# Retention in a hybrid trunk: values and gates of two heads in one product of 512 columns, and the first head's output transposes behind the next pair's query

## The chip, the core and the metric

The kernel runs on one core of a Trainium2 chip. A core has TensorE (PE, matmuls; its weight loads are shown apart as PEld), VectorE (DVE), ScalarE (ACT), GpSimd (POOL) and SyncE (SP, which here only issues transfers). The engines run side by side, each through its own instructions in order, and wait for each other by semaphores. SBUF is the working memory, PSUM the eight banks of 512 float32 a partition into which PE writes. The metric is the time of one execution on the device in microseconds (us).

## What is computed

The program is one inference step of a trunk of four layers (S5, retention, Hyena, S5) over 128 context tokens and 256 latent tokens, 1024 wide, in float32. The change lies in the retention layer alone, which has 8 heads of 128 query and key dimensions and 256 value dimensions:

```python
def retention_branch(h, s0, grid_pos, w_in, decay_logit, w_out):
    proj = h @ w_in                       # 1024 -> 1024 + 1024 + 2048 + 2048
    q, k, v, gate = jnp.split(proj, [RET_QK, 2 * RET_QK, 2 * RET_QK + RET_V], axis=-1)
    ...
    o_f, s_f = retention_chunkwise(q, k, v, lg[0], s0[:, 0], True)
    o_b, s_b = retention_chunkwise(q[:, ::-1], k[:, ::-1], v[:, ::-1], lg[1], s0[:, 1], False)
    o = o_f + o_b[:, ::-1]
    o = o * lax.rsqrt(jnp.mean(o * o, axis=-1, keepdims=True) + EPS)
    out = (o.reshape(bsz, L, RET_V) * jax.nn.silu(gate)) @ w_out
```

## The kernel before

All dense products are made in three parts: weights and activations are each split into a rounded value (h) and its remainder (l) of a reduced float32 type, and `mm` (L138 to L141) adds the products hh, hl and lh in PSUM. `unit` (L158 to L166) makes the two parts of 1024 weight elements a partition: ACT casts (L164), and the remainder is taken by POOL in one of three cases (through the helper at L136) and by DVE otherwise (L151). There are two buffers of each part. `weight` (L153 to L156) loads 1 MB on SP's queue into one of two buffers.

There are two ways to lay out a product. `featmajor` holds the weights in the array and moves 384 tokens through it: 24 matmuls a unit, one PSUM bank. `tokmajor` holds 128 tokens of the activation in the array and moves 256 weight columns through it, for three blocks of tokens at once: it takes all three banks of the pool `psd`, and a unit of 4 blocks of the contraction by 256 columns feeds 36 matmuls.

The retention layer goes through its heads in four pairs (`hp`). For a pair, queries and keys of both heads come first (four chunks by `featmajor`, `qk_chunk`), then values and gates by `tokmajor` (`vg_chunk`): value of the first head, gate of the first, value of the second, gate of the second, each with one 1 MB load and two units. A value is copied out of PSUM by ACT (L1086), a gate goes through a tanh on ACT (L533) and a product on DVE (L534) in `silu2`.

Between these chunks stand the steps of `head`: `scores` (products of q and k in two passes of float32, L1015 to L1023, masks by DVE into A, the key's transpose scaled into kk, L1020, and the loads of E, QD and the state s0 on SP's queue, L1006 to L1009); `values` (A times v and the scaled query times the state, L1031 to L1038, the norm's squares on ACT and its steps on DVE, L1043 to L1049, which write zt; and the new state from kk and v, L1053); and `turn` (six transposes of zt, L1061, copied by ACT into the blocks z that the output projection reads). kk, zt, s0 and QD have one buffer, the scores' A and E two. PSUM for these steps comes from the pool `psm` of four banks.

After each chunk stands a `tick`, which takes one task from a list of background work: one block of operators of the last S5 layer (`both`: expansions on DVE (L631, L632) and POOL (L636), small products L668 and transposes L674 into `psm`, and stores to scratch, among them that of CP, which has one buffer here), or nothing.

The second head's `values` and `turn` of a pair run behind the first two query chunks of the next pair (the list `late`), those of the last pair around the first steps of the output projection `OutProj`, which reads all blocks z.

The program's text isn't the order of execution: a planner goes through it with a model of times and takes for each engine the earliest instruction that is ready in the model, so that waiting chunks let later steps pass. On the chip each engine then keeps to the planned order.

Of the kernel before, what the change touches and what calls it, by code (L numbers as in the profile page):

```python
# [10 lines left out]
F32 = mybir.dt.float32  # L11
# [6 lines left out]
D = 1024  # L18
NB = D // 128
# [11 lines left out]
DV = 256  # L31
# [76 lines left out]
def hybrid_trunk(ctx: ExitStack, tc: tile.TileContext, I, O, dbg=None, layers=(0, 1, 2, 3)):  # L108
# [44 lines left out]
    def weight(src):  # L153
        raw = wraw.tile(list(src.shape), F32, tag="wr", name="wr")
        nc.sync.dma_start(raw, src)
        return raw  # L156
# [32 lines left out]

    def tokmajor(raw, act, epi):  # L190
        pss = [psd() for _ in range(3)]
        for k0 in range(0, NB, 4):
            w = unit(raw[:, k0:k0 + 4, :])
            for t in range(3):
                for kb in range(4):
                    mm(pss[t][:, :256], [p[:, k0 + kb, t * 128:(t + 1) * 128] for p in act],
                       [p[:, kb, :] for p in w], k0 + kb == 0, k0 + kb == NB - 1)
        for t in range(3):
            epi(t, pss[t][:, :256])

# [734 lines left out]
    def retention(i, zpool, hpool, nxt):  # L935
# [130 lines left out]
        for hp in range(4):  # L1066
# [15 lines left out]

            def vg_chunk(nm, m):
                o = vg[nm, m] = rot.tile([128, 3, DV], F32, tag=nm, name=nm)
                tokmajor(weight(W[(8 if nm == "v" else 16) + 2 * hp + m]), h,
                         lambda t, ps: S.copy(o[:, t, :], ps) if nm == "v" else silu2(o[:, t, :], ps))  # L1086

# [7 lines left out]
            if hp == 0:  # L1095
                z += [zblock(zpool, F32) for _ in range(16)]
            vg_chunk("v", 0)
            heads[0][0]()
            tick()
            vg_chunk("g", 0)  # L1100
            heads[1][0]()
            tick()
            vg_chunk("v", 1)
            heads[0][1]()
            tick()
            vg_chunk("g", 1)
            heads[0][2]()
            tick()
            late = [heads[1][1], heads[1][2]]
        drain()  # L1110
        op = OutProj(I["ret_w_out"], z, zpool, hpool)
        late[0]()
        op.split(0, 14)
        op.part(0, 0, 8)
        op.part(0, 8, 14)
        late[1]()
        op.part(1, 0, 8)
# [372 lines left out]
def _layout(a):  # L1490
    ca = np.ascontiguousarray
    o = {}
# [34 lines left out]
    qk = w[:, :2 * D].reshape(D, 16, 2, 2, 2, 16).transpose(0, 1, 2, 4, 3, 5).reshape(D, 2 * D)  # L1527
    o["ret_w_in"] = _slabs(np.concatenate([qk, w[:, 2 * D:]], 1), 256)
    o["ret_w_out"] = _slabs(a["ret_w_out"][0], 128)
# [48 lines left out]
```

## Time and profile before

| | us |
|---|---|
| median of three runs | 1631.56 |
| lowest and highest | 1630.19, 1633.9 |
| the profiled execution | 1632.28 |
| its span, first to last instruction | 1630.5 |
| PE, DVE, ACT, POOL busy | 1449.2, 1246.0, 692.2, 664.3 |

The busy time of PE counts a matmul from its start to its modelled end; matmuls overlap, so the distance from one start to the next is what a matmul costs in a stream. A wait in the views below is idle time of the waiting engine just before an instruction, named by what ended it; where a semaphore counts all instructions of an engine, the name may be that of a neighbour of the true cause. Retention's pairs run from about 456 to 757 us.

### The profile page before, as it was taken

The numbers are of one execution on the slowest core, as the hardware profiler recorded it, in microseconds if no ns is written. First come the engines' busy times: TensorE is split into PE (matmuls) and PEld (weight loads), VectorE is DVE, ScalarE is ACT, GpSimd is POOL, SyncE is SP. The second block draws the span as 40 slices with busy tenths as digits, with TensorE's granted clock in tenths as the row PEclk, the third lists the DMA queues.
The fourth block names the chain that finished last, engine by engine and source line by source line (L and its number), as shares of the span: only waits on it lengthen the run. The fifth ranks groups of instructions, "written<-read, shape, count | busy, mean of one in ns | idle before, by whom it ended". The sixth has DMA issues, their size and how long they took to land. (4 is left out here: it accounts for less than half of the span.)

```text
span 1630.5 us, 27608 instructions
## 1 busy us (share of the span) xinstructions
PE 1449.2 (89%) x10370; PEld 1280.7 (79%) x10370; DVE 1246.0 (76%) x2935; ACT 692.2 (42%) x1275; POOL 664.3 (41%) x484
## 2 busy tenths in 40 slices
PE   6778787798799899999979999999999999988996
PEld 3555585577588888889968988999998898767886
DVE  8966998699886767755968887888888874379565
ACT  2434522244333333334445544546445534542443
POOL 2111242325374857551225665655666332132221
PEclk9887899899799999999989999999999999999998
DMA  9487499843555555543333322322322345577531
GB/s 359 130 260 224 150 222 253 284 178 128 216 173 179 183 207 187 183 154 130 127 125 101 101 78 75 101 84 95 100 78 94 106 174 201 167 217 196 199 130 65
DMA packets 107805, 261.39 MB, mean 160 GB/s; under 512 B 28535, under 2 KB 68568, under 8 KB 88088
## 3 DMA queue, kind: packets, MB, share of 16 engines
q1 hardware_dynamic: 80768, 200.12, 37.2%
q0 software_dynamic: 11984, 34.87, 7.7%
q10 hardware_dynamic: 14920, 24.65, 4.3%
q8 instruction: 82, 1.34, 0.3%
q14 instruction: 51, 0.42, 0.1%
HBM read 220.37 MB, written 30.83 MB: 154 GB/s over the span
## 5 line engine op out<-in xcount | busy, mean ns | idle before, releaser
L136 POOL TENSOR_TENSOR wl<-wr,wh 128x1024 fp32r<-128x1024 f32 (+2 forms) x99 | 248.9, 2515 | 300.2 <-ACT wh L164 273.6
L164 ACT CAST wh<-wr 128x1024 fp32r<-128x1024 f32 (+4 forms) x211 | 215.7, 1028 | 315.0 <-PE psd L141 200.5
L141 PE MATMUL psd<-hh,wh 128*128 128x384 f32 x880 | 307.3, 350 | 13.5 <-DVE X L798 7.0
L141 PE MATMUL psd<-hl,wh 128*128 128x384 f32 x880 | 305.7, 347 | 6.4 <-DVE hl L472 6.2
L141 PE MATMUL psd<-hh,wl 128*128 128x384 f32 x880 | 305.3, 347 | 4.7 <-POOL wl L136 2.6
L151 DVE TENSOR_TENSOR wl<-wr,wh 128x1024 fp32r<-128x1024 f32 (+3 forms) x112 | 147.2, 1315 | 71.9 <-ACT wh L164 71.5
L141 PEld LDWEIGHTS psd<-hh,wh 128*128 128x128 f32 x880 | 169.7, 193 | 26.6 <-issue 14.5
L141 PEld LDWEIGHTS psd<-hl,wh 128*128 128x128 f32 x880 | 169.9, 193 | 15.9 <-DVE hl L472 8.9
L141 PEld LDWEIGHTS psd<-hh,wl 128*128 128x128 f32 x880 | 169.7, 193 | 12.2 <-issue 5.1
L141 PE MATMUL psd<-wl,hh 128*128 128x256 f32 x384 | 110.0, 288 | 4.0 <-POOL wl L136 2.0
L141 PE MATMUL psd<-wh,hh 128*128 128x256 f32 x384 | 110.0, 292 | 2.6 <-ACT k L1077 1.6
L141 PE MATMUL psd<-wh,hl 128*128 128x256 f32 x384 | 109.0, 286 | 0.0
L381 PE MATMUL psn<-wr,sgc 128*32 128x256 f32 x640 | 58.3, 460 | 35.0 <-DMA wr<-in_mod_w_dram 23.9
L141 PE MATMUL psd<-zb,wh 128*128 128x384 f32 x240 | 80.9, 338 | 0.0
L141 PEld LDWEIGHTS psd<-wl,hh 128*128 128x128 f32 x384 | 74.1, 193 | 6.3 <-POOL wl L136 3.2
L141 PEld LDWEIGHTS psd<-wh,hh 128*128 128x128 f32 x384 | 73.3, 193 | 4.5 <-ACT k L1077 2.0
L636 POOL TENSOR_TENSOR BP<-BP,xt 128x512 f32<-128x512 f32 x32 | 47.3, 1479 | 71.9 <-DVE xt L632 36.4
L141 PEld LDWEIGHTS psd<-wh,hl 128*128 128x128 f32 x384 | 74.1, 193 | 0.1
L631 DVE TENSOR_TENSOR CP<-B,xc 128x512 f32<-128x512 f32 x52 | 52.9, 1044 | 26.5 <-DMA scratch_cpd_dram<-CP 15.6
L632 DVE TENSOR_TENSOR xt<-BI,xc 128x512 f32<-128x512 f32 x52 | 47.2, 909 | 29.6 <-POOL CP L636 17.2
L381 PEld LDWEIGHTS psn<-wr,sgc 128*32 128x32 f32 x640 | 20.0, 124 | 56.9 <-DMA wr<-in_mod_w_dram 27.8
L797 DVE TENSOR_TENSOR X<-X,m 128x64 f32<-128x64 f32 x184 | 64.2, 349 | 0.0
(385 smaller groups left out, 3843.1 us busy)
## 6 DMA issues: line engine op xcount, KB each, us to landing
wr<-in_mod_w_dram SPq DMA_DIRECT2D x40, 1024.0 KB
wr<-in_hy_w_in_dram SPq DMA_DIRECT2D x32, 1024.0 KB
wr<-in_ret_w_in_dram SPq DMA_DIRECT2D x24, 1024.0 KB
wr<-in_s_w_in_dram SPq DMA_DIRECT2D x16, 1024.0 KB
wm<-in_mod_w_dram SPq DMA_DIRECT2D x8, 1024.0 KB
CP<-xt POOLq DMA_DIRECT2D x32, 256.0 KB, 7.2
Tt<-scratch_kd_dram SPq DMA_DIRECT2D x128, 64.0 KB
wr<-in_s_w_glu_dram SPq DMA_DIRECT2D x8, 1024.0 KB
```

The costliest lines, as they stand in the source:

```text
L136: G.tensor_tensor(out, a, b, op=op)
L141: TE.matmul(out, lhs[a], rhs[b], start=start and i == 0, stop=stop and i == len(combos) - 1)
L151: V.tensor_sub(out, a, b)
L164: S.copy(hi, ap)
L381: TE.matmul(ps[q * 32:(q + 1) * 32, :256], sg[:, kb, 6 - 2 * u:38 - 2 * u], raw[:, kb, :], start=u == 0 and k2 == 0, stop=u == 3 and k2 == 1)
L631: eng.tensor_tensor(out, c1, x[:, 0].unsqueeze(2).to_broadcast([128, 4, 8, 16]), op=OP.mult)
L632: eng.tensor_tensor(t, c2, x[:, 1].unsqueeze(2).to_broadcast([128, 4, 8, 16]), op=OP.mult)
L636: add.tensor_tensor(out, out, t, op=OP.add)
L797: V.tensor_add(dst, dst, m1[:, 0])
```

## The change

Values and gates are made for both heads of a pair at once. The weights' slabs hold 512 columns; a `tokmajor` chunk loads them in two halves of 1 MB, and a unit is 2 blocks of the contraction by 512 columns, which feeds 18 matmuls of 512 columns. There are two chunks a pair instead of four; v and g have one buffer of double width instead of two. The first head's scores stand ahead of the value chunk, the second head's behind it; the first head's values stand behind the gate chunk, and its `turn` moves to behind the first query chunk of the next pair. The four ticks stay four, one behind the value chunk, one behind the second head's scores, one behind the gate chunk, one behind the first head's values.

```diff
-    def tokmajor(raw, act, epi):
+    def tokmajor(src, act, epi):
         pss = [psd() for _ in range(3)]
-        for k0 in range(0, NB, 4):
-            w = unit(raw[:, k0:k0 + 4, :])
+        for k0 in range(0, NB, 2):
+            if k0 % 4 == 0:
+                raw = weight(src[:, k0:k0 + 4, :])
+            w = unit(raw[:, k0 % 4:k0 % 4 + 2, :])
             for t in range(3):
-                for kb in range(4):
-                    mm(pss[t][:, :256], [p[:, k0 + kb, t * 128:(t + 1) * 128] for p in act],
+                for kb in range(2):
+                    mm(pss[t], [p[:, k0 + kb, t * 128:(t + 1) * 128] for p in act],
                        [p[:, kb, :] for p in w], k0 + kb == 0, k0 + kb == NB - 1)
         for t in range(3):
-            epi(t, pss[t][:, :256])
+            epi(t, pss[t])
...
-            def vg_chunk(nm, m):
-                o = vg[nm, m] = rot.tile([128, 3, DV], F32, tag=nm, name=nm)
-                tokmajor(weight(W[(8 if nm == "v" else 16) + 2 * hp + m]), h,
-                         lambda t, ps: S.copy(o[:, t, :], ps) if nm == "v" else silu2(o[:, t, :], ps))
+            def vg_chunk(nm):
+                o = rot.tile([128, 3, 2 * DV], F32, tag=nm, name=nm, bufs=1)
+                for m in range(2):
+                    vg[nm, m] = o[:, :, m * DV:(m + 1) * DV]
+
+                def epi(t, ps):
+                    if nm == "v":
+                        S.copy(o[:, t, :], ps)
+                        return
+                    for m in range(2):
+                        silu2(vg[nm, m][:, t, :], ps[:, m * DV:(m + 1) * DV])
+                tokmajor(I["ret_w_vg"][hp + (0 if nm == "v" else 4)], h, epi)
...
-            vg_chunk("v", 0)
             heads[0][0]()
+            vg_chunk("v")
             tick()
-            vg_chunk("g", 0)
             heads[1][0]()
             tick()
-            vg_chunk("v", 1)
+            vg_chunk("g")
+            tick()
             heads[0][1]()
             tick()
-            vg_chunk("g", 1)
-            heads[0][2]()
-            tick()
-            late = [heads[1][1], heads[1][2]]
+            late = [heads[0][2], heads[1][1], heads[1][2]]
         drain()
         op = OutProj(I["ret_w_out"], z, zpool, hpool)
         late[0]()
+        late[1]()
         op.split(0, 14)
         op.part(0, 0, 8)
         op.part(0, 8, 14)
-        late[1]()
+        late[2]()
...
-    o["ret_w_in"] = _slabs(np.concatenate([qk, w[:, 2 * D:]], 1), 256)
+    o["ret_w_in"] = _slabs(qk, 256)
+    o["ret_w_vg"] = _slabs(w[:, 2 * D:], 512)
```

## Rows read from the trace of the kernel before

**Rows 1.** The page: engines' busy time, share of the span, instructions.
```profile
PE 1449.2 (89%) x10370; PEld 1280.7 (79%) x10370; DVE 1246.0 (76%) x2935; ACT 692.2 (42%) x1275; POOL 664.3 (41%) x484
```
**Rows 2.** Busy time by stretch: what follows the pairs, and all four pairs.
```profile
core 0: us, PE busy (x) PEld busy (x) DVE busy (x) ACT busy (x) POOL busy (x), PEclk, DMA share, GB/s
...
757.00:780.00 23.00, 23.00 (x132) 22.00 (x131) 15.17 (x31) 13.25 (x28) 6.49 (x7) 1.00 0.52 162
456.00:757.00 301.00, 279.29 (x2079) 258.49 (x2078) 206.25 (x375) 112.00 (x254) 173.97 (x129) 0.99 0.53 177
```
**Rows 3.** PE's groups, 456 to 757 us: count | busy us, mean ns | idle, releasers.
```profile
L141 PE MATMUL psd<-wl,hh 128*128 128x256 f32 x384 | 110.0, 288 | 4.0 <-POOL wl L136 2.0 <-DVE wl L151 1.9
L141 PE MATMUL psd<-wh,hh 128*128 128x256 f32 x384 | 110.0, 292 | 2.6 <-ACT k L1077 1.6 <-DVE g L534 1.1
...
L674 PE MATMUL psm<-ident,BP 128*128 128x128 f32 x112 | 16.7, 280 | 7.9 <-DVE A L1026 3.1 <-DVE kk L1020 2.2 <-DVE nr L284 1.1
```
**Rows 4.** PE's waits, 456 to 757 us: total us, times, longest.
```profile
PE psd L141 <- POOL wl L136: 4.6, 5, 1.5
PE psd L141 <- DVE g L534: 3.4, 4, 2.3
...
PE psd L141 <- DVE wl L151: 1.9, 2, 1.0
```
**Rows 5.** PE's timeline, 256 columns: start us, us, instruction.
```profile
573.13 0.28 PE L141 MATMUL psd<-wl,hh 128*128 128x256 f32 x1
...
574.57 0.28 PE L141 MATMUL psd<-wl,hh 128*128 128x256 f32 x1
```
**Rows 6.** PE's timeline, 384 columns.
```profile
599.63 0.33 PE L141 MATMUL psd<-hh,wh 128*128 128x384 f32 x1
...
601.19 0.33 PE L141 MATMUL psd<-hh,wh 128*128 128x384 f32 x1
```
**Rows 7.** PE's timeline, a head's values, each product two passes (x2).
```profile
577.97 0.59 PE L1038 MATMUL psm<-v,A 128*128 128x256 f32 x2
578.40 0.59 PE L1035 MATMUL psm<-s,qf 128*128 128x256 f32 x2
```
**Rows 8.** PE's timeline, its idle time in brackets with what ended it.
```profile
565.13 0.39 PE L141 MATMUL psd<-wh,hh 128*128 128x256 f32 x1 [0.30 <-DVE g L534]
...
595.69 0.44 PE L141 MATMUL psd<-hh,wh 128*128 128x384 f32 x1 [2.33 <-DVE g L534]
...
655.63 0.66 PE L674 MATMUL psm<-ident,BP 128*128 128x128 f32 x4 [2.24 <-DVE A L1026]
```
**Rows 9.** A gate's way out of PSUM, groups from 456 to 757 us.
```profile
L534 DVE SCALAR_TENSOR_TENSOR g<-silu,psd 128x256 f32<-128x256 f32 x24 | 9.5, 412 | 7.7 <-ACT silu L533 7.7
...
L533 ACT ACTIVATE silu<-psd 128x256 f32<-128x256 f32 x24 | 8.4, 379 | 9.7 <-PE psd L141 9.3 <-PE psm L1061 0.4
```
**Rows 10.** DVE's timeline, then PE's, at one late bank.
```profile
501.82 1.29 DVE L631 TENSOR_TENSOR CP<-B,xc 128x512 f32<-128x512 f32 x2 [4.20 <-DMA scratch_cpd_dram<-CP]
...
504.90 0.66 PE L674 MATMUL psm<-ident,BP 128*128 128x128 f32 x4 [1.86 <-DVE kk L1020]
```
**Rows 11.** PE's and DVE's timeline, from a head's values to its zt.
```profile
580.13 1.03 PE L1053 MATMUL psm<-v,kk 128*128 128x256 f32 x4
...
587.78 1.27 DVE L1049 SCALAR_TENSOR_TENSOR zt<-psm,rrs,g 128x256 f32<-128x256 f32 x3
```
**Rows 12.** The granted clock falls: one stretch, then PE's timeline.
```profile
620.00:622.00 2.00, 2.00 (x8) 2.00 (x8) 2.00 (x2) 0.13 (x1) 2.00 (x3) 0.50 0.90 360
...
618.33 0.44 PE L141 MATMUL psd<-hh,wl 128*128 128x384 f32 x1 [1.50 <-POOL wl L136]
...
620.35 0.52 PE L141 MATMUL psd<-hl,wh 128*128 128x384 f32 x1
620.67 0.52 PE L141 MATMUL psd<-hh,wl 128*128 128x384 f32 x1
```
**Rows 13.** SP's queue, 456 to 757 us: waits of the state's load.
```profile
SPq L1009 <- PE psm L1036: 19.1, 5, 9.5
```

## Prediction

> **What bounds the kernel now.** I read the page first: TensorE (PE) is busy 89% of the span, VectorE (DVE) 76%, the other two about 40% [rows 1]. An average over different stages says little about one stage, so the next view is the table by stretch. It is cut here at the four pairs of heads of the retention stage: from 456 to 757 us PE is busy 279.29 of 301.00 us, DVE 206.25, GpSimd (POOL) 173.97, ScalarE (ACT) 112.00, and from 757 on, when the output projection runs, PE is full [rows 2]. So in this stage PE sets the pace, and 21.7 us of it are idle. Third, PE's groups by shape: the 1152 matmuls with 256 moving columns are the largest item, 384 for each of three products of 110 us each; two of the three rows stand in [rows 3]. Those durations are no cost: a matmul lasts 288 ns in the trace, but the next starts long before it ends. What counts is the distance of starts, and for that one needs the timeline. Fourth, PE's waits in this stretch say where the idle 21.7 us lie [rows 4].
>
> **Part 1: 512 moving columns.** From 573.13 to 574.57 us twelve steps of 256 columns take 1.44 us, 120.0 ns a step [rows 5]. From 599.63 to 601.19 nine steps of 384 columns take 1.56 us, 173.3 ns [rows 6]. Both lie at full granted clock (2.4 GHz, 0.4167 ns a column): 256 columns are 106.7 ns and 384 are 160.0. The remainder is 13.3 ns in both, so it belongs to the instruction and not to the column. No matmul of 512 columns stands in the trace, so I extend the line: 213.3 + 13.3 = 226.7 ns, an estimate from those two rows. The change turns 1152 x 120.0 = 138.2 us into 576 x 226.7 = 130.6 us: **-7.7 us**. Bounds: a remainder of 2.9 ns, as of the retention's own two-pass products (0.433 us for two passes of 256 columns that move at two clocks a column, 216.3 ns each) [rows 7], gives 576 x (240.0 - 216.2) = -13.7 us; a remainder that doubles with the columns gives 0. I take the middle value, since its rows have the same line, operands and type.
>
> The Trainium skill says otherwise: "TensorE: Matmul & The Clock Gate", section "Back-to-back issue gap", gives N / 2.4 + 2.5 ns for a stream at full clock, and by an estimate from that the 256 columns would step in 109.2 ns, a pair of them would lose 2.5 ns by being joined, and the whole change would be worth 1.4 us. The trace disagrees at 256 and at 384 columns (120.0 and 173.3 ns), and the measurement decides for these; at 512 no run here shows which holds, so it returns as a rival.
>
> **Part 2: the weights' halves.** There are 32 units of 1024 elements as before, cast by ACT with the remainder by DVE or POOL as before, and 16 loads of 1 MB as before. A unit now feeds 18 matmuls, 4.08 us, instead of 36, 4.32 us. Where the unit's remainder comes late, that shorter stretch is no gain: PE just waits 0.24 us longer. Of the seven waits on remainders, 6.5 us in all [rows 4], 4.0 us stand ahead of 256-column products [rows 3], five of them at most; I give back 5 x 0.24 = **+1.2 us** (bounds 0 and 7.7, if every unit came late).
>
> **Part 3: fewer hand-overs of PSUM banks.** A chunk takes all three banks at once. PE waited 3.4 us in four times for a gate's evacuation [rows 4]. 1.1 us of that stand ahead of 256-column products [rows 3], that is at the border from the first head's gate to the second head's value; the row at 565.13 shows one of 0.30 [rows 8]. That border is gone: **-1.1 us**. The fourth, 2.33 us, stands between a gate chunk and the next pair's query [rows 8], and this border stays. There a bank now needs two tanh (379 ns) and two products (412 ns) instead of one each [rows 9], 0.8 us more; the first bank closes 12 x 0.2267 = 2.7 us ahead of the chunk's end, which hides that unless DVE is behind. The value's copies become half as many and twice as wide: nothing on the path, as ACT is busy 112 of 301 us [rows 2]. If each of the four gates ran into a wait of 2.33, this would be +7.0.
>
> **Part 4: scores ahead of the value chunk.** The first head's scores now come right behind the keys. They are some 1.2 us of PE (four passes of 256, two of 128 and a transpose), and they give ACT that much more to free the key's bank; PE waited 1.6 us there [rows 3]. I take half, **-0.8 us** (0 to -1.6). The scores' three loads (E, QD, s0) move on SyncE's queue, too: the first head's ahead of the value's weights, the second head's between value and gate. s0 has one buffer, so the second head's s0 waits for the first head's L1036, which now lies behind the whole gate chunk; queued behind it are the weights of the next pair's query. The queue waited so for 19.1 us in five times before, 9.5 at most [rows 13], and the view of PE's waits names no load [rows 4], as two weight buffers lie between: 0, and up to 9.5 a time if the query's weights were planned behind s0.
>
> **Part 5: what is bunched.** Four ticks of background work (a block of the last layer's operators each) still fall to the values and gates of a pair, but they come two by two with a head's step between, behind 16.3 us of matmuls, and no longer one by one behind 8.6 us. The transposes of that work (L674) need PSUM banks of the pool of four. PE waited 7.9 us there, for score products A 3.1, for kk 2.2, for a norm step 1.1 [rows 3]. Two things get tighter. kk has one buffer: the second head's kk must wait for the first head's state product (L1053), and until then its scores' bank is held. Between the two lay one chunk of 8.6 us, now one of 16.3. And DVE works in order: at 501.82 it had waited 4.20 us for the scratch store of CP before it could go on; kk stood behind that, and PE got its bank at 504.90, 1.86 us late [rows 10]. I take a quarter more of 7.9, **+2.0 us**, with bounds of -3 (the order comes out better) and +8 (all of it doubles).
>
> **Part 6: the transposes behind the next query.** For three pairs nobody reads z until the output projection: 0. They share zt with the second head, whose zt is written a chunk later. In the last pair the transposes stand at the end, behind the norm chain: state product from 580.13, zt until 589.05, about 8 us later [rows 11]. Beside it lie the second head's values (22 passes of 216 ns, 4.8 us), and the first 24 products of the output projection (24 x 0.1733 = 4.2 us), which read other blocks: 9.0 us. So 0, and 3.8 us if only one of the two covers it.
>
> **Sum.** -7.7 + 1.2 - 1.1 - 0.8 + 2.0 = -6.4 us. The profiled execution took 1632.28 us (span 1630.5), 0.7 above the median of 1631.56, so it is 1625.9 by that execution and **1625.2** by the median.
>
> **Rivals.**
> A. The remainder is not an instruction's. If only 2.9 ns, as of the two-pass products [rows 7], were the instruction's and the other 10.4 came again with every 256 columns, a product of 512 would take 213.3 + 2.9 + 20.8 = 237.0 ns, a gain of 3.0 x 576 = 1.7 us, and with the other terms (+1.3) the time would be about 1631.2. Against it: 256 and 384 columns have the same remainder. For it: nothing in the trace is wider than 386 columns, and at the lower clock level 384 columns step in 320 ns, 384 / 1.2 without any remainder [rows 12], so that it isn't an instruction's at all times. The rule of the Trainium skill's page named above would give nearly this time, too (1.4 us in place of 1.7).
> B. **The new bunches cost more than the matmuls give.** Place: DVE's queue behind each pair's value chunk, where CP of the second tick waits for the store of the first, and kk and the remainder stand behind. Price: the 4.20 us of [rows 10], not partly but wholly on PE, once a pair: 4 x 4.20 = 16.8, and 1625.2 + 16.8 = 1642. It decides from 6.4 / 4 = 1.6 us a pair, less than the 2.24 us that one such wait cost at 655.63 [rows 8]. For it: DVE is busy 69% of the stage and POOL 58% [rows 2]. Against it: the planner sees the same buffers and can put the two ticks apart.
> C. The remainder is smaller at 512 columns and less is bunched (+1.0 for part 5): -13.7 + 1.2 - 1.1 - 0.8 + 1.0 = -13.4, about 1618.
> D. A term of its own: soon after a wait of 1.50 us the granted clock stood at 0.50, its lower level of 1.2 GHz, from 620 to 622 us; 384 columns then step in 320 instead of 173.3 ns, so these 2 us hold 6.3 products instead of 11.5 and lose 0.9 us [rows 12]. Such a loss may vanish or come two or three times; it moves any case by that.
>
> **How the numbers follow.** Forecast 0.50 (1621 to 1629), A 0.13, B 0.20 (from little over 1632 to 1642), C 0.17. Of the forecast I count 0.43 beyond 0.2% (3.3 us, about what a measurement of this kernel can tell from no change) and 0.07 within; C is all beyond; A is within; of B 0.03 is within and 0.17 beyond. So faster 0.60, same 0.23, slower 0.17. The range goes from 1617 (C and a little) to 1637 (half of B's price); it leaves out some 0.07 below and 0.10 above.
>
> **What would show it.** Right: steps of 226 to 228 ns between 512-column products; 576 fewer matmuls; the stretch from the first value chunk to the output projection shorter by 5 to 8 us; PE's idle time in it about 22 us, with fewer waits on g. Wrong: steps of 216 (C) or 237 to 240 ns (A); waits of L674 on kk, A or a norm step of 15 us and more (B); PE idle at the start of the output projection, where it is full from 757 to 780 us now (part 6). If the sum fails, I expect it in part 5, whose size is the least known.

## The result, and the profile after

The changed kernel takes 1648.16 us (median of 4 runs, 1642.76 to 1654.99) beside 1632.39 for the kernel before (median of 4): a ratio of 1.0107, 95% interval 1.0082 to 1.0132. It is slower by 15.8 us where 6.4 less were forecast, and lies 11 us above the upper end of the range. Its profiled execution took 1654.99 us with a span of 1653.2; it is the slowest of the four, and 22.7 us longer than the profiled execution of the kernel before.

The page after: each engine's busy time, share of the span and instructions (beside [rows 1]):

```profile
PE 1457.7 (88%) x9794; PEld 1256.5 (76%) x9794; DVE 1251.1 (76%) x2935; ACT 692.9 (42%) x1263; POOL 670.9 (41%) x484
```

There are 576 matmuls fewer, as the change says (10370 to 9794), and yet PE is busy for longer. To see where, I cut the stage at landmarks that both kernels have. The *pairs* go from the first value product to the end of the last gate or value product; the *tail* from there to the start of the 110th `psd<-zb,wh` product of the output projection; the *rest* from there to the end. The table by stretch, first the kernel before, pairs and tail (start:end, length, then each engine's busy us and instructions, granted clock, DMA share, GB/s):

```profile
core 0: us, PE busy (x) PEld busy (x) DVE busy (x) ACT busy (x) POOL busy (x), PEclk, DMA share, GB/s
459.54:750.83 291.29, 269.58 (x2026) 249.25 (x2026) 197.00 (x360) 105.06 (x236) 170.68 (x126) 0.99 0.53 179
750.83:816.62 65.79, 65.50 (x366) 62.77 (x364) 54.05 (x97) 33.31 (x64) 14.30 (x14) 1.00 0.39 131
```

The same two stretches after:

```profile
461.44:756.00 294.56, 269.56 (x1447) 219.17 (x1446) 206.38 (x346) 102.69 (x216) 171.64 (x127) 0.97 0.53 177
756.00:834.93 78.93, 68.98 (x366) 65.23 (x367) 55.47 (x111) 35.14 (x72) 15.57 (x13) 0.91 0.32 109
```

Pairs and tail together are 373.49 us where they were 357.08: +16.4, about as much as the medians differ (15.8). (The two profiled executions differ by 6.3 us more, ahead of the stage and behind it.) Of the 16.4, +3.3 lie in the pairs and +13.1 in the tail, for the same 366 matmuls there. PE's idle time (length less busy) goes from 21.7 to 25.0 us in the pairs and from 0.3 to 10.0 in the tail: +12.9. The tail was the stretch where the prediction had PE full [rows 2].

The wide products themselves, groups of PE from 456 to 790 us (count, busy us, mean ns, idle time ahead of them; beside [rows 3]):

```profile
L141 PE MATMUL psd<-wl,hh 128*128 128x512 f32 x192 | 80.0, 417 | 6.8 <-DVE wl L151 4.6 <-POOL wl L136 2.1
L141 PE MATMUL psd<-wh,hh 128*128 128x512 f32 x192 | 73.3, 414 | 5.7 <-ACT wh L164 4.0 <-ACT k L1079 1.6
...
L676 PE MATMUL psm<-ident,BP 128*128 128x128 f32 x120 | 18.5, 283 | 0.3 <-DVE nr L287 0.3
```

and their distance, from PE's timeline, the first and the last of thirteen steps:

```profile
752.66 0.39 PE L141 MATMUL psd<-wh,hl 128*128 128x512 f32 x1
...
755.61 0.39 PE L141 MATMUL psd<-wh,hl 128*128 128x512 f32 x1
```

2.95 us for thirteen steps are 226.9 ns, as forecast. PE's waits, 456 to 790 us (total, times, longest; beside [rows 4]):

```profile
PE psm L1063 <- DVE zt L1051: 12.8, 2, 9.0
PE psd L141 <- DVE wl L151: 4.9, 6, 1.8
PE psd L141 <- DVE g L536: 4.1, 2, 2.7
PE psd L141 <- ACT wh L164: 4.0, 1, 4.0
PE psm L1033 <- DVE Kc L682: 2.3, 1, 2.3
PE psd L141 <- POOL wl L136: 2.1, 2, 1.4
```

The first line is new: L1063 are the transposes that the change moved. 9.0 us of the 12.8 are in the tail, the other 3.7 in the pairs:

```profile
720.37 0.48 PE L1063 MATMUL psm<-ident,zt 128*128 128x128 f32 x2 [3.73 <-DVE zt L1051]
```

PE's timeline in the tail (idle time in brackets, with what ended it):

```profile
751.57 1.02 PE L1055 MATMUL psm<-v,kk 128*128 128x256 f32 x4
...
756.37 0.45 PE L141 MATMUL psd<-zhh,wh 128*128 128x384 f32 x1 [0.38 <-ACT zhh L247]
765.85 0.69 PE L1063 MATMUL psm<-ident,zt 128*128 128x128 f32 x2 [9.03 <-DVE zt L1051]
766.33 1.06 PE L1033 MATMUL psm<-v,A 128*128 128x256 f32 x2
...
774.05 0.52 PE L141 MATMUL psd<-zb,wh 128*128 128x384 f32 x1
```

The transposes wait for zt at the head of PE's queue, and what should have covered that wait stands behind them: the second head's values (from 766.33) and the output projection (from 774.05, one product excepted). And zt is late because of ScalarE's queue in the same stretch:

```profile
755.81 2.16 ACT L247 CAST zhh<-zb 128x384 fp32r<-128x384 f32 x5 [0.51 <-PE psd L141]
757.88 0.64 ACT L535 ACTIVATE silu<-psd 128x256 f32<-128x256 f32 x2
758.42 1.33 ACT L247 CAST zhh<-zb 128x384 fp32r<-128x384 f32 x3
759.64 1.75 ACT L247 CAST zhl<-zb 128x384 fp32r<-128x384 f32 x4
761.29 0.83 ACT L164 CAST wh<-wr 128x768 fp32r<-128x768 f32 x1
762.03 0.38 ACT L535 ACTIVATE silu<-psd 128x256 f32<-128x256 f32 x1
762.30 0.38 ACT L1045 ACTIVATE junk<-psm 128x256 f32<-128x256 f32 x1
```

The squares (L1045), first link of the norm chain, run at 762.30, although the values that they read closed at about 751: six silu (the first three at 753.77 and 754.64), twelve casts for the output projection and a weight cast are planned ahead of them. VectorE ends the chain:

```profile
765.31 1.27 DVE L1051 SCALAR_TENSOR_TENSOR zt<-psm,rrs,g 128x256 f32<-128x256 f32 x3
```

**The clock** adds to that. The stretches of the stage with the lower of the two levels, 1.2 GHz, after:

```profile
495.25:498.75 3.50, 3.50 (x9) 2.75 (x10) 2.32 (x4) 2.02 (x3) 1.48 (x1) 0.52 0.90 251
625.00:632.00 7.00, 5.17 (x17) 3.69 (x20) 6.89 (x13) 1.32 (x2) 4.10 (x4) 0.51 0.25 96
679.75:683.00 3.25, 3.25 (x12) 3.25 (x12) 2.41 (x11) 1.51 (x8) 0.00 (x0) 0.50 0.39 103
720.75:724.00 3.25, 3.25 (x24) 2.08 (x24) 1.52 (x3) 1.31 (x4) 0.00 (x0) 0.50 0.31 48
758.25:771.75 13.50, 5.90 (x17) 4.91 (x18) 9.95 (x28) 7.40 (x23) 0.00 (x0) 0.50 0.07 21
```

and before (the first is that of [rows 12]):

```profile
619.25:622.75 3.50, 3.50 (x13) 3.50 (x12) 3.17 (x4) 0.28 (x1) 3.50 (x3) 0.52 0.91 300
656.75:660.25 3.50, 3.50 (x19) 3.50 (x18) 1.54 (x4) 1.21 (x2) 3.20 (x3) 0.51 0.71 253
```

If half of PE's busy time in these is lost, an estimate, that is 21.1 / 2 = 10.5 us after and 7.0 / 2 = 3.5 before. Together: idle +12.9, clock +7.0, and 16.4 - 12.9 - 7.0 = -3.5 is left for the work. So the wide products did give something, and two other things took more than five times as much.

### The profile page after: what moved, and what is told of

Read it like the earlier page. It is cut to its first block, busy times and chain, and to the rows that moved or that the text cites. A ratio compares the mean times of both kernels' runs of the same rounds, so it can differ in the third digit from the quotient of the medians.

```text
span 1653.2 us, 26440 instructions
## 1 busy us (share of the span) xinstructions
PE 1457.7 (88%) x9794; PEld 1256.5 (76%) x9794; DVE 1251.1 (76%) x2935; ACT 692.9 (42%) x1263; POOL 670.9 (41%) x484
## 5 line engine op out<-in xcount | busy, mean ns | idle before, releaser
L164 ACT CAST wh<-wr 128x1024 fp32r<-128x1024 f32 (+4 forms) x211 | 215.8, 1029 | 349.2 <-PE psd L141 218.8
L141 PE MATMUL psd<-wl,hh 128*128 128x512 f32 x192 | 80.0, 417 | 6.8 <-DVE wl L151 4.6
L141 PE MATMUL psd<-wh,hh 128*128 128x512 f32 x192 | 73.3, 414 | 5.7 <-ACT wh L164 4.0
L141 PE MATMUL psd<-wh,hl 128*128 128x512 f32 x192 | 77.0, 401 | 0.0
L638 POOL TENSOR_TENSOR BP<-BP,xt 128x512 f32<-128x512 f32 x32 | 50.8, 1587 | 60.2 <-DVE xt L634 39.1
L634 DVE TENSOR_TENSOR xt<-BI,xc 128x512 f32<-128x512 f32 x52 | 46.9, 904 | 26.8 <-POOL BP L638 12.8
L633 DVE TENSOR_TENSOR BP<-F,bc 128x512 f32<-128x512 f32 x64 | 55.0, 866 | 13.9 <-PE psm L676 11.7
L633 DVE TENSOR_TENSOR CP<-B,xc 128x512 f32<-128x512 f32 x52 | 48.6, 960 | 18.4 <-DMA xc<-in_s5bc_dram 11.4
L636 POOL DMA_DIRECT2D CP<-xt x32 | 27.9, 918 | 81.6 <-DVE xt L634 41.0
L634 DVE TENSOR_TENSOR xt<-FI,bc 128x512 f32<-128x512 f32 x64 | 50.7, 792 | 12.9 <-POOL BP L638 8.1
L638 POOL TENSOR_TENSOR CP<-CP,xt 128x512 f32<-128x512 f32 x32 | 46.2, 1445 | 34.8 <-DVE xt L634 22.5
```

Source lines behind the costliest of these rows:

```text
L141: TE.matmul(out, lhs[a], rhs[b], start=start and i == 0, stop=stop and i == len(combos) - 1)
L164: S.copy(hi, ap)
L633: eng.tensor_tensor(out, c1, x[:, 0].unsqueeze(2).to_broadcast([128, 4, 8, 16]), op=OP.mult)
L634: eng.tensor_tensor(t, c2, x[:, 1].unsqueeze(2).to_broadcast([128, 4, 8, 16]), op=OP.mult)
L636: nc.gpsimd.dma_start(out, t, accum_op=OP.add)
L638: add.tensor_tensor(out, out, t, op=OP.add)
```

## The experiments

Totals are a poor judge here: the stretch ahead of the stage, whose order of work is the same in all, took 452.9 to 466.8 us in 20 profiles. Pairs and tail repeat better (two profiles each of before, of the change and of e12 agree within 1.3, 1.8 and 3.0 us), so I read those first. All profiles, in us; "idle" is PE's in pairs and tail:

```
kernel             ratio to before, 95%      pairs   tail  idle   rest
before                                       291.3   65.8  22.0  813.9
b2_before_again    1.0004 (0.9977, 1.0030)   292.5   65.8  21.4  813.9
after              1.0107 (1.0082, 1.0132)   294.6   78.9  34.9  818.3
a1_changed_again   1.0137 (1.0102, 1.0171)   297.5   77.8  36.0  813.1
e1_move_only       1.0093 (1.0069, 1.0117)   298.0   67.7  25.5  815.0
e2_turn_back       1.0057 (1.0030, 1.0085)   283.9   77.5  27.8  816.9
e3_last_pair_old   1.0109 (1.0067, 1.0151)   295.9   67.7  26.7  816.7
e4_order_only      1.0088 (1.0053, 1.0123)   290.8   77.5  31.1  812.8
e6_later           1.0046 (1.0016, 1.0077)   294.7   72.3  29.1  813.6
e7_gf_later        1.0032 (0.9998, 1.0066)   285.9   75.9  27.2  815.6
e8_before_later    1.0056 (1.0029, 1.0084)   297.5   67.9  28.6  815.0
e9_ticks_spread    1.0087 (1.0055, 1.0118)   296.4   78.0  38.2  812.1
e10_all            1.0078 (1.0047, 1.0108)   286.0   75.8  28.1  812.3
e11_v_first        1.0096 (1.0064, 1.0128)   300.4   69.4  34.7  811.8
e12_both           1.0035 (1.0012, 1.0057)   284.9   67.6  21.1  820.9
e13_order_256      1.0022 (1.0001, 1.0043)   287.5   67.9  20.0  816.0
e14_tail_only      1.0032 (1.0010, 1.0055)   284.5   70.7  21.4  819.3
e15_gate_first3    1.0006 (0.9984, 1.0027)   287.3   67.8  21.5  814.6
e16_two_pairs      1.0057 (1.0032, 1.0083)   295.7   67.6  29.1  814.9
e17_both_again     1.0030 (1.0006, 1.0055)   287.6   67.9  21.5  817.6
```

The tails hold 360 to 375 products; those of e7 and e10 hold 389 (part of the first head's values falls behind the border), some 4 us of work that their pairs don't have.

### The two kernels again

a1 is the changed kernel unaltered, b2 the kernel before.

> The changed kernel once more, with a second profile, since its four times lie between 1642.8 and 1655.0 us and the trace read so far is that of the slowest. Theory T1 (the end of the stage): the wait of the first head's transposes in the last pair, 9.0 us in the first profile, stands in this one too, between 8 and 10 us, and the low clock behind it; what differs between the runs lies elsewhere. Theory T2 (bunched background work in the order of VectorE and ScalarE): the waits inside the pairs differ from run to run and sum up to more than the end. Time 1642 to 1655.

> The kernel before, unchanged: a second profile of it, to see how far the stage from the first value chunk to the output projection, its idle time and its low-clock time scatter from one execution to the next. The first profile had 357.6 us, 22.0 us and 6.8 us there. If these scatter by under 3 us, differences of 6 us between single profiles of variants carry weight; if by 6 or more, they don't. Time as before, ratio 1.000 within 0.003.

Measured: 1650.71 us and 1632.22 us. Pairs plus tail repeat within 1.8 and 1.3 us and idle time within 1.1 and 0.7, so a difference of 6 us between two profiles' stages counts.

### e1_move_only and e4_order_only: either half of the change with 256 columns

e1 is the kernel before with the transposes moved and nothing else:

```
-            heads[0][2]()
             tick()
-            late = [heads[1][1], heads[1][2]]
+            late = [heads[0][2], heads[1][1], heads[1][2]]
...
         late[0]()
+        late[1]()
...
-        late[1]()
+        late[2]()
```

e4 is the change with each joined chunk as two chunks of 256 columns, one behind the other (in short):

```
-                tokmajor(I["ret_w_vg"][hp + (0 if nm == "v" else 4)], h, epi)
+                for m in range(2): tokmajor(weight(W[(8 if nm == "v" else 16) + 2 * hp + m]), h, ...)
```

> The kernel before with 256 columns and four chunks, only the first head's transposes moved behind the next pair's first query chunk. In the last pair the second gate chunk (8.6 us) still stands between the first head's values and its transposes. T1: no wait at the end, 1632 (1630 to 1636, at most the 3.7 us that the moved transposes cost inside a pair). T2: 1632, as nothing is bunched. If the move itself were the loss: 1640 or more.

> The changed kernel's order (both values, then both gates, scores and ticks placed the same, transposes moved) with products of 256 columns, so 1152 matmuls at 120 ns. If the step per instruction is what the 512 columns save: the changed kernel + 7.7 us = 1656 (1650 to 1660). If the wide products themselves make the loss: 1632 to 1636. T1: a wait of some 9 us for the transposes at the end here too.

Measured: 1644.92 and 1642.60 us. e1 came out by its third case, that the move itself is a loss; e4 lies between its two. The table by stretch of e1 and its waits:

```profile
460.85:758.83 297.98, 274.54 (x2025) 255.44 (x2025) 211.69 (x360) 106.19 (x236) 174.51 (x126) 0.96 0.53 175
758.83:826.51 67.68, 65.61 (x366) 62.87 (x365) 54.03 (x97) 33.10 (x64) 15.03 (x14) 1.00 0.37 125
```
```profile
PE psm L1061 <- DVE zt L1049: 6.8, 2, 4.1
PE psm L674 <- DVE zt L1049: 4.5, 1, 4.5
...
PE psm L674 <- DVE nr L284: 3.1, 1, 3.1
```

The same two stretches of e4, and its transposes in the tail:

```profile
457.87:748.64 290.77, 268.36 (x2016) 247.18 (x2016) 210.30 (x347) 104.51 (x229) 168.34 (x128) 0.99 0.55 180
748.64:826.13 77.49, 68.85 (x375) 65.34 (x374) 57.18 (x111) 35.40 (x71) 15.41 (x14) 0.96 0.33 112
```
```profile
758.21 0.69 PE L1061 MATMUL psm<-ident,zt 128*128 128x128 f32 x2 [7.66 <-DVE zt L1049]
```

So the tail is lost without a single wide product (e4, 77.5), and it is nearly whole with the transposes moved but the chunks in their old order (e1, 67.7). With the moved transposes, what loses it is the order of the chunks: both heads' gates directly ahead of the first head's values, so that silu and casts stand ahead of the squares. And the move, which the prediction priced at nothing inside the pairs, costs 6.7 us there (298.0 against 291.3). Only 1.7 us of that is more idle time; 5.0 us is PE being busy for longer (274.54 against 269.58) at the lower clock, which covers 23.9 us of e1's pairs and 6.8 before.

### e3_last_pair_old and e2_turn_back: one part undone with 512 columns

e3 does the last pair in the order of the kernel before (256 columns), the other three as in the change (in short):

```
+            if hp < 3:
...
+            else:
+                vg_old("v", 0); heads[0][0](); tick(); vg_old("g", 0); heads[1][0](); tick()
+                vg_old("v", 1); heads[0][1](); tick(); vg_old("g", 1); heads[0][2](); tick()
```

e2 is the change with the transposes called at the pair's end again:

```
             heads[0][1]()
+            heads[0][2]()
             tick()
-            late = [heads[0][2], heads[1][1], heads[1][2]]
+            late = [heads[1][1], heads[1][2]]
...
```

> The changed kernel with the last of the four pairs done as before (four chunks of 256 columns, transposes at the pair's end). T1: the 9 us of waiting at the end and some 2.4 us of half clock behind it go, 1.9 us of matmul gain of that pair go too: 1648 - 11.4 + 1.9 = 1639 (1634 to 1643). T2: three of four pairs keep their bunches: 1648 - 16/4 = 1644 or more.

> The changed kernel with one part undone: the first head's transposes stand right behind its values again, at the end of the pair, in place of behind the next pair's first query products. In the last pair the order of TensorE's work comes out as in the changed kernel. Theory 1 (the transposes' wait for zt in TensorE's queue is the loss): the wait in the last pair of about 9 us stays, the one of 3.7 us inside the pairs goes or moves with the transposes; 1644 to 1650. Theory 2 (the bunched background work is the loss): nothing of it is changed, 1648 to 1650. So this run tells mainly whether the place of the transposes in the program text matters at 512 columns.

Measured: 1647.35 and 1643.49 us. e3's tail is 67.7 us, 11 less than the change's, as theory 1 said; its pairs stay at 295.9. (Its time does not show that: 1640.98 in the profiled run, 1647.35 in the median.) e2's tail stays at 77.5, and its pairs are shorter than in either kernel:

```profile
465.70:749.63 283.93, 266.14 (x1447) 216.74 (x1446) 208.74 (x346) 103.02 (x216) 170.65 (x127) 0.98 0.56 183
749.63:827.09 77.46, 67.50 (x367) 64.19 (x367) 55.38 (x111) 35.16 (x72) 15.58 (x13) 0.93 0.32 111
```

7.4 us less than before and 10.6 less than the change. That the transposes' place doesn't matter is out for the pairs. For the tail e2 says nothing about it: the planner brings the last pair's transposes to the same place there, PE's order through the tail is that of the change, and the wait is again 9.03 us. e14 below moves them in the tail.

### e6_later, e8_before_later, e7_gf_later: the transposes later still

If waiting for zt were the loss, more distance would repair it. All three write zt in place of the gates, so that each head has its own, and call the transposes later; e6 is so made from the change, e8 from the kernel before, e7 from the change with gate and value chunk exchanged:

```
-            late = [heads[0][2], heads[1][1], heads[1][2]]
+            late = [heads[1][1], heads[0][2], heads[1][2]]
...
+        op.split(0, 12)
+        op.part(0, 0, 8)
+        op.part(1, 0, 8)
         late[1]()
...
```

> The changed kernel with the first head's transposes later still: behind the next pair's second query products (zt is written in place of the gates, so that both heads have one of their own), and in the last pair behind the first 48 products of the output projection, whose blocks 0 to 11 are split first. The 512 columns and the bunched background work stay. Theory 1 (transposes wait for zt in TensorE's in-order queue, with matmuls behind them, and the low clock follows): waits on zt fall from 12.8 to under 2 us, and with some 4 us of low clock the time falls to 1630 to 1636. Theory 2 (bunched background work): waits on weights, gates and casts stay near 15 us and low clock too; 1643 to 1650.

> The kernel before (256 columns, its order of chunks) with the same later place of the first head's transposes. The move alone, to directly behind the first query products, gave 1644.9. Theory 1 (distance between the values and the transposes decides): 1629 to 1634, waits on zt under 2 us where the move alone had 11. Theory 2 (any new order of this stage lands some 10 us worse, whatever the transposes wait for): 1640 to 1646.

> As the run before it (transposes later), and the gate chunk ahead of the value chunk, so that the norm chain of the first head's values does not stand behind the six silu pairs on ScalarE and VectorE. Theory 1: waits on zt under 1 us, 1627 to 1634. Theory 2: background ticks fall at the same places, 1643 to 1650. If it comes out below the kernel before, the 512 columns' 3 to 8 us are seen.

Measured: 1639.43, 1642.15 and 1639.71 us. e8's time is theory 2's; those of e6 and e7 lie between the two. Theory 1 falls for the pairs. e8 shows no wait of the transposes at all and its pairs are 297.5 us, as long as e1's; e6's waits on zt are down to 3.8 us and its pairs are as long as the change's (294.7). e7's 285.9, with the gates first, is some 4 us too short by the border (see above): it comes to about 290. The idle time has moved to other waits: in e8 12.8 us on weights' remainders where [rows 4] has 6.5. So with the moved step the pairs are 3 to 6 us longer than before even where it waits little or not at all itself. That it changes what stands ahead of what on VectorE, ScalarE and POOL is my reading; no run isolates it (zt moved into the gates, too).

### e9_ticks_spread, e10_all, e11_v_first: part 5 of the prediction

e9 is the change with one tick in the middle of each joined chunk (`half` in its loop) and one behind each:

```
+            if half and k0 == 2:
+                half()
```

e10 is e7 with that, e11 is e6 with that.

> The changed kernel, only its ticks of background work put back to one per eight microseconds: one in the middle and one behind each joined chunk, in place of two by two behind each. The transposes stay where the change put them. Theory 1 (transposes waiting for zt): the waits on zt of 9 to 13 us stay and the time is 1646 to 1650. Theory 2 (bunched background work, part 5 of the prediction): waits on weights' remainders, gates and casts fall from 15 to 8 us, time 1636 to 1640.

> 512 columns with all suspects treated at once: ticks spread as in the run before, gate chunk ahead of the value chunk, transposes behind the second query products, and in the last pair behind the first 48 products of the output projection. If transposes' waits, bunched ticks and the silu ahead of the squares are the whole loss, the wide columns' own gain is left, some 4 us: 1626 to 1630. If merging the chunks costs in another way (weights' remainders, granted clock), it stays at 1636 to 1641, as with late transposes and gate first but bunched ticks (ratio 1.003).

> As the run before it, with the value chunk ahead of the gate chunk, as in the change. If the order of the two chunks matters by itself (six silu pairs between values and norm chain), 4 us slower than that run and waits on g of 3 us or more; if not, within 3 us of it.

Measured: 1644.56, 1642.82 and 1643.93 us. e9 keeps the waits on zt (9.7 us), as theory 1 has it; its waits on remainders, gates and casts fall from 15.1 to 11.8 us, but those on k rise from 1.6 to 6.9. e10 lies above both of its cases. Spreading the ticks gives the change nothing (374.4 us of pairs and tail against 373.5 and 375.3), nor e7 (361.7 against 361.8). e11's time is within 1.1 us of e10's, but its stage is 8 us longer; the order of the two chunks matters there.

### e12_both, e13_order_256, e14_tail_only: both losses undone

e12 is e2 in three pairs and e3 in the last. e13 is e12 with 256 columns, edited as e4, and so prices the columns. e14 is e2 in three pairs and e6 in the last, 512 columns throughout:

```
             heads[0][1]()
+            if hp < 3:
+                heads[0][2]()
             tick()
+            late = [heads[1][1]] + [heads[0][2]] * (hp == 3) + [heads[1][2]]
```

> 512 columns in the first three pairs, with the first head's transposes back at the pair's end, and the last pair wholly in the order of the kernel before (256 columns, single chunks). If the loss is the two places where transposes wait (inside the pairs and at the last pair), what is left is three quarters of the columns' gain: the pairs end some 6 us earlier than before, the end of the stage is as before; 1625 to 1628 by a median of 1631 for before. Rival (merging chunks costs in another way, seen in every variant so far at ratios of 1.003 to 1.01): 1635 to 1640.

> The run before it with 256 columns: two chunks of 256 one behind the other in place of each joined one, all else the same. If 227 against 2 x 120 ns a step is the whole of the columns' worth, 432 x 13.3 ns = 5.7 us longer than that run in the stage, so 1631 to 1634. If the joined chunks cost as much in waits as they give in steps, no difference.

> 512 columns in all four pairs, transposes back at the pair's end in three of them; in the last pair they stand behind the first 48 products of the output projection (zt is written in place of the gates). If the place of the transposes is the whole loss of the last pair, 1625 to 1629; if the silu work ahead of the squares and the values of both heads at the end cost by themselves (6 us more matmul and evacuation work is then behind the last chunk), 1632 to 1638.

Measured: 1634.74, 1634.94 and 1635.27 us: near the rival's case for e12, no difference for e13, the second case for e14. In e12 the stage is 4.6 us shorter than before, near what was expected, and the time is not. Pairs, tail and rest of e12, and the pairs of e17, which is e12 once more:

```profile
462.93:747.78 284.85, 265.78 (x1593) 223.66 (x1593) 212.91 (x360) 105.45 (x227) 169.30 (x126) 0.99 0.55 183
747.78:815.43 67.65, 65.62 (x368) 62.88 (x366) 53.80 (x97) 33.09 (x64) 15.02 (x14) 1.00 0.36 125
815.43:1636.30 820.87, 761.73 (x5173) 696.33 (x5172) 612.67 (x1312) 388.49 (x650) 346.82 (x220) 0.97 0.37 123
```
```profile
458.12:745.70 287.58, 268.36 (x1593) 226.72 (x1593) 212.46 (x360) 105.78 (x227) 168.90 (x126) 0.98 0.55 181
```

The pairs of e13, and the tail of e14:

```profile
462.94:750.40 287.46, 269.77 (x2025) 250.17 (x2025) 216.92 (x360) 106.16 (x236) 167.42 (x126) 0.99 0.54 182
```
```profile
740.58:811.30 70.72, 67.57 (x368) 64.16 (x366) 54.45 (x111) 34.77 (x72) 15.21 (x14) 0.98 0.34 119
```

At the same granted clock PE is busy 4.0 us less in e12's pairs: 432 wide steps in place of 864, 9.2 ns each, close to what the steps give. The pairs are only 2.6 us shorter than e13's, and those of e17, with more of the lower clock, not at all (287.58); e13's are 3.8 us shorter than before without any wide product. So most of what e12 gains in the pairs is the new order's, and what the columns give in length is not clear of the scatter.

e14 settles the tail. Its chunks stand as in e2, but zt is written into the gates, and in the last pair 48 products of the output projection are queued ahead of the transposes: no wait on zt is left in the tail, PE idles 3.2 us there in place of 10.0, and the tail is 70.7 us in place of 77.5. So the chunks' order makes zt late, and the transposes' place in PE's queue makes PE wait for it; the loss needs both.

Behind the stage e12 loses 7.0 us, at places that no edit touched. There PE's order is another one from the 99th instruction behind the tail on: the next layer's filter products stand earlier, and wait. PE's waits of e12 from 815 to 870 us:

```profile
PE psm L461 <- DVE dg L460: 5.2, 1, 5.2
PE psm L1267 <- ACT ab L1259: 2.3, 1, 2.3
```

Before has the first of these, too, but not the second.

### e15_gate_first3, e16_two_pairs, e17_both_again: was it the order behind the stage?

e15 is e12 with gate and value chunk exchanged in the first three pairs, e16 is e12 with only the first and the third pair joined; in both, PE's order behind the stage is that of the kernel before for over 4000 instructions. e17 is e12 once more. The edits of e15 and of e16 against e12:

```
-                vg_chunk("v")
+                vg_chunk("g")
...
-                vg_chunk("g")
+                vg_chunk("v")
```
```
-            if hp < 3:
+            if hp in (0, 2):
```

> 512 columns in three pairs with the gate chunk ahead of the value chunk in these, the transposes at the pair's end, the last pair as in the kernel before. TensorE's order behind the stage is that of the kernel before. If the new order behind the stage was what cost 7 us in the run with both repairs, then here the stage is 353 to 356 us, the remainder behind it 812 to 815, and the time 1626 to 1630. If the remainder is longer whatever its order, 1633 to 1636.

> The run with both repairs, with 512 columns in the first and the third pair alone. Order behind the stage as in the kernel before. 288 steps of 512 columns at 2 x 119.7 - 229.2 = 10.2 ns less give 2.9 us: stage 354 to 356, remainder 812 to 815, time 1628 to 1630; 1633 to 1636 if the order behind the stage is not the cause.

> The run with both repairs again, unchanged. If its stage and its remainder belong to the kernel and not to the one execution, 351 to 355 us and 817 to 821 us; time 1632 to 1637.

Measured: 1632.35, 1640.57 and 1636.27 us. The rest is 814.6 and 814.9 us with the old order, 820.9 and 817.6 with the new one. The other profiles, sorted by that order, agree: the nine with the order of before for over 4000 instructions (before, b2, e6, e8, e9, e11, e13, e15, e16) have 811.8 to 816.0 us behind the tail, the four with e12's (e3, e12, e14, e17) 816.7 to 820.9, and the seven with others (the change's among them, which part from before at about the 133rd instruction) 812.3 to 818.3. That makes e12's order worth some 4 to 5 us by the medians, where one and the same kernel scatters by up to 5.2 (the change). Of the mechanism the new wait is shown, 2.3 to 2.7 us in all four, and the clock (0.84 from 815 to 870 us in e12, where before has 0.91 in its 55 us there); the remainder I can't name. e15's stage and rest came out as expected for the old order, though its time lies between its two cases; e17 came out within 0.5 us of what was expected. e16 missed for another reason: its pairs take 295.7 us with 27.0 of idle time, though e12 has both kinds of pair, too. e15 is the best version found: 2.0 us shorter than before in pairs and tail, and in time the same as the kernel before (1.0006, 0.9984 to 1.0027). No version beat it.

## Why the prediction was wrong

**Part 1 was right in the step and some 2 us too large in its worth.** The step is 227 ns (median of the undisturbed ones), close to the forecast 226.7, and rival A with its 237.0 is out. The rule cited beside rival A, of the Trainium skill's "TensorE: Matmul & The Clock Gate", section "Back-to-back issue gap", would by an estimate from its formula give 215.8 ns for 512 columns; the trace disagrees (227). The same section says that the formula is off for a stream with a weight load ahead of each matmul, which is what runs here. The mean of the undisturbed steps is 229.0 ns (steps of 231 to 236 are frequent), against 119.7 for 256: 576 x 10.4 = 6.0 us, where I had 7.7 from 226.7 for every step. In PE's busy time the balance of the stage above leaves 3.5, and e12 against e13 gives 4.0 for three pairs of four.

**Parts 2 to 4** were small and stay small. Waits on remainders: 6.5 to 7.0 us (+1.2 forecast). Waits on gates: 3.4 to 4.1 (-1.1 forecast): the one border that stays now costs more, as its own bound had it. Waits on k: 1.6 as before (-0.8 forecast). The scores' loads, priced at 0, name no wait of PE.

**Part 5, where I expected the sum to fail, held at the place that it named, and rival B's mechanism did not come.** The transposes L674 (now L676) waited 7.9 us before [rows 3] and 0.3 us after, where I had +2.0; no wait on kk or on A stands in PE's list, and VectorE's waits for the store of CP fell from 15.6 to 5.8 us (456 to 790 us). But the background work made PE wait at places that part 5 did not name: 2.3 us behind Kc, and 4.0 us behind a weight cast that ScalarE could not reach, as it waited 9.07 us for the load of a background block (`bc`) first:

```profile
621.36 0.51 ACT L653 ACTIVATE bc<-bc,sgn 128x256 f32<-128x256 f32 x1 [9.07 <-DMA bc<-in_s5bc_dram]
...
622.96 1.06 ACT L164 CAST wh<-wr 128x1024 fp32r<-128x1024 f32 x1
...
624.07 1.00 PE L141 MATMUL psd<-wh,hh 128*128 128x512 f32 x2 [3.99 <-ACT wh L164]
```

The longest low stretch of the pairs follows it (625 to 632 us), and a1 has this wait, too (3.3 us). Whether the bunching causes it is not shown: in e9, with the ticks spread, it is gone, but other waits take its place and the time stays.

**Part 6 is the step that failed, at both places where I wrote 0.** For three pairs I wrote that "nobody reads z until the output projection: 0". True of the data, and beside the point: PE takes its work in order, so a transpose that waits holds the matmuls behind it, whoever reads its result. In the trace that is one wait of 3.73 us at 720.37, with low clock from 720.75 on; undoing the move is worth 10.6 us in the pairs with wide columns (e2), and making it costs 6.7 without (e1), more of that through the lower clock than through idle time. e6 and e8 show that the transposes' own wait is only part of it. The working also overlooked that `late` is taken one entry a chunk: with a third entry ahead, the second head's values and transposes move one chunk later, too.

For the last pair I named a cover of 9.0 us (second head's values and 24 products) and "3.8 us if only one of the two covers it". Neither did: both stood behind the transposes in PE's queue, and with 48 products ahead of them (e14) the wait is gone. And the chain from the state product to zt, "about 8 us" in the forecast and 8.9 from start to end in [rows 11], took from 751.57 to 766.58, 15.0 us, since its length was taken from a pair in which ScalarE had no gate chunk of two heads and no casts for the output projection ahead of the squares. I asked which work could lie beside the wait, and not in which order the queues hold it.

**D was mis-sized.** I gave the clock 0.9 us per occurrence and two or three of these; by the estimate above the loss went from 3.5 to 10.5 us in the stage. The price came from 2 us of a stretch that lasts 3.5 (619.25 to 622.75) and so costs 1.75. In this trace the five low stretches all begin soon after a wait (of 2.32 us at 495.13, 3.99 at 624.07, 2.66 at 678.43, 3.73 at 720.37) or within one (the 9.03). No fixed price per us of waiting follows: e4 idles 9 us more than before with no more loss by the clock (3.1 us by the same estimate), e1 only 3.5 more with 10.8, and e12 and e17, one kernel, have 3.1 and 6.8.

**The upper end of the range** does not follow from its reason: 1625.2 and half of B's 16.8 us are 1633.6, not 1637, which is the middle between B's 1632 and 1642. The measured 1648.16 lies beyond all of these.

**One assumption stood nowhere in the working:** that what lies behind the stage stays as it is. For the change itself two profiles disagree (818.3 and 813.1); e3, e12, e14 and e17, with 816.7 to 820.9, show that it needn't.

**What stays open.** Why the pairs take 284 to 288 us in some of the kernels tried and 294 to 300 in others. It is the order and not chance (the idle time of before, of the change and of e12 repeats within 1.1 us). One edit sorts nearly all: the five kernels at 284 to 288 (e2, e12, e13, e14, e15; e7 and e10 only by the border) have the two value and the two gate chunks side by side and the first head's transposes at the pair's end, in the first three pairs; all with the transposes moved in these are at 290 or above. e16 does not fit: its transposes are at the pair's end, and it takes 295.7. The idle time is spread over waits of 1 to 4 us on remainders, gates, casts, expansions and kk, other ones in each, so which queue carries the cost of the move is not shown. Taking away ScalarE's wait for `bc` ahead of the cast at 624.07 was not tried.

## What to carry to other kernels

Before a step is moved in an in-order queue, list what stands behind it there and what stands ahead of its inputs on the other engines; whether anyone needs its result is the smaller question, and a cover counts only if it is queued ahead of the wait. A merge of two chunks doubles what the evacuating engine has in front of the next chain (here six silu in place of three), which is paid where the cover ends, here in the last pair. And where a planner orders the whole program, judge an edit by stretches between landmarks in the trace, and look behind the stage as well: a few us gained in it can be given back where nothing was edited.

## What the chip showed that I had not expected

The distance of matmuls does not have one value at full clock: with 512 columns 226 to 228 ns are the commonest and 231 to 236 frequent, while nearly all steps of 256 columns keep to 116 to 121. At the lower clock the two-pass products of the values, 216 ns a pass at full clock [rows 7], take 428 (768.04 to 769.75 us, four passes). And one and the same order of work ahead of the stage took 452.9 to 466.8 us from run to run, more than all that was at stake here.
